# Row normalisation on Trainium2: the size of the DMA descriptors of its loads and stores

## The chip, the cores and the metric

The kernel runs on one core of one Trainium2 chip. The metric is the device time of one launch in microseconds (us). The kernel before the change took 316.64 us as the median of 3 runs (316.41 to 316.7).

## The reference

The input is `x`, 32 x 512 x 1024 numbers in float32 (67.11 MB). Each row of 1024 numbers is divided by the sum of its absolute values:

```python
sums = np.sum(np.abs(x), axis=-1, keepdims=True)
return (x / (sums + 1e-8)).astype(np.float32)
```

Every number is read once and written once, so 134.22 MB must move between the memory (HBM) and the on-chip buffer (SBUF).

## The kernel before

The input is flattened to 16,384 rows of 4,096 bytes. There are 128 SBUF partitions, so each handles 128 rows in all. The rows are cut into eleven tiles: tiles 0 to 9 hold 12 rows per partition (49,152 bytes per partition, 6.29 MB per tile), and tile 10 holds 8 rows per partition (32,768 bytes per partition, 4.19 MB). `piece` (line 33) says which rows a tile holds. Tiles 0, 1 and 10 together are the first 4,096 rows of the input, 32 successive rows per partition; each other tile is a block of 1,536 successive rows, 12 per partition. In every tile the bytes of one partition are contiguous in HBM and in SBUF.

There are four tile buffers (`BUFS = 4`, line 27), and a tile is normalised in place: it is loaded, computed on and stored from the same buffer. The order of the work is written out by hand (lines 108 to 115). Loads of tiles 0 to 3 are issued first. Then, for each tile in turn, `compute(i)` and `store(i)` are issued, and after them `load(i + 4)`, which has to wait until store `i` has landed, because it writes into the same buffer.

Three engines take part:

- SyncE (SP) issues the loads, on its own DMA queue (q1 in the profile), at line 87.
- VectorE (DVE) sums the absolute values of each row (`tensor_reduce`, line 47), adds the epsilon (line 54), takes the reciprocal (line 56) and multiplies most rows (lines 58 and 65).
- ScalarE (ACT) multiplies a few rows of tiles 0, 1, 2, 9 and 10 (line 68) and issues the stores, on its own DMA queue (q10 in the profile), at line 97.

Both queues feed the same 16 DMA engines. A tile is spread evenly over them: 8 of the 128 partitions fall to each engine.

A DMA is made of descriptors, each of which moves one contiguous stretch of bytes; the profile counts and times each of them as one packet, and this text uses that word. `max_dma_last_dim` sets how long, in bytes, such a stretch may be. `HALF` (24,576) is six rows, `WHOLE` (49,152) is twelve rows, and `4 * d` (4,096) is one row. A tile of 12 rows is therefore 128 packets with `WHOLE` and 256 packets with `HALF`; tile 10, with 8 rows, is 128 packets of 32,768 bytes with `WHOLE` and 256 of 16,384 with `HALF`.

The store of tile 0 is issued in two parts: rows 0 to 2 as soon as they are ready, one row per packet (384 packets), and then rows 3 to 11 (128 packets of 36,864 bytes). The store of tile 8 (`last - 2`) is issued in two parts of six rows each, which are 128 packets of 24,576 bytes each whether the limit is `HALF` or `WHOLE`.

In this text "load 4" is the load of tile 4, "store 0a" and "store 0b" are the two parts of the store of tile 0, and "store 8a" and "store 8b" those of tile 8.

Of the kernel before, what the change touches and what calls it, by code (L numbers as in the profile page):

```python
# [1 line left out]

# [4 lines left out]

FP32 = mybir.dt.float32
EPS = 1e-8


@with_exitstack
def kernel(
    ctx: ExitStack,
    tc: tile.TileContext,
    x: bass.AP,
    out: bass.AP,
):
    nc = tc.nc
    P = nc.NUM_PARTITIONS  # L20

    x_flat = x.flatten_outer_dims()
    out_flat = out.flatten_outer_dims()
    n, d = x_flat.shape

    R = 12
    BUFS = 4
    HEAD = 32
    per_partition = n // P
    assert n % P == 0 and (per_partition - HEAD) % R == 0  # L30
    rows = [R] * ((per_partition - HEAD) // R + 2) + [HEAD - 2 * R]

    def piece(flat, i):
        head = flat[: P * HEAD, :].rearrange("(p r) d -> p r d", p=P)
        if i < 2:
            return head[:, R * i : R * (i + 1), :]
        if i == len(rows) - 1:
            return head[:, 2 * R :, :]
        a = P * (HEAD + R * (i - 2))
        return flat[a : a + P * R, :].rearrange("(p r) d -> p r d", p=P)  # L40

    sbuf = ctx.enter_context(tc.tile_pool(name="sbuf", bufs=BUFS))
    stats = ctx.enter_context(tc.tile_pool(name="stats", bufs=len(rows)))

    def normalize(x_tile, k, kv, kt):
        s = stats.tile([P, R], FP32)
        nc.vector.tensor_reduce(  # L47
            out=s[:, :k],
            in_=x_tile[:, :k, :],
            axis=mybir.AxisListType.X,  # L50
            op=mybir.AluOpType.add,
            apply_absolute_value=True,
        )
        nc.vector.tensor_scalar_add(out=s[:, :k], in0=s[:, :k], scalar1=EPS)  # L54
        inv = stats.tile([P, R], FP32)
        nc.vector.reciprocal(out=inv[:, :k], in_=s[:, :k])  # L56
        if kv:
            nc.vector.tensor_mul(  # L58
                out=x_tile[:, :kv, :],
                in0=x_tile[:, :kv, :],  # L60
                in1=inv[:, :kv].unsqueeze(2).to_broadcast([P, kv, d]),
            )
        for r in range(kv, kv + kt):
            row = x_tile[:, r, :]
            nc.vector.tensor_scalar_mul(out=row, in0=row, scalar1=inv[:, r : r + 1])  # L65
        for r in range(kv + kt, k):
            row = x_tile[:, r, :]
            nc.scalar.activation(  # L68
                out=row,
                in_=row,  # L70
                func=mybir.ActivationFunctionType.Copy,
                scale=inv[:, r : r + 1],
            )

    last = len(rows) - 1
    split = {0: (3, 4), 1: (0, 3), 2: (0, 3), last - 1: (0, 2), last: (4, 4)}

    tiles = {}

    HALF, WHOLE = 24576, 49152
    FIRST = 3

    def load(i):
        x_tile = tiles[i] = sbuf.tile([P, R, d], FP32, name="x_tile")
        nc.sync.dma_start(out=x_tile[:, : rows[i], :], in_=piece(x_flat, i), max_dma_last_dim=WHOLE if i < 2 else HALF)  # L87

    def store(i):
        if i == 0:  # L90
            parts = [(0, FIRST, 4 * d), (FIRST, R, WHOLE)]
        elif i == last - 2:
            parts = [(0, R // 2, HALF), (R // 2, R, HALF)]
        else:
            parts = [(0, rows[i], WHOLE if i >= last - 1 else HALF)]
        for a, b, size in parts:
            nc.scalar.dma_start(
                out=piece(out_flat, i)[:, a:b, :],
                in_=tiles[i][:, a:b, :],
                max_dma_last_dim=size,  # L100
            )

    def compute(i):
        k = rows[i]
        kt, ks = split.get(i, (0, 0))
        normalize(tiles[i], k, k - kt - ks, kt)

    with tc.manual_schedule():
        for i in range(BUFS):
            load(i)  # L110
        for i in range(len(rows)):
            compute(i)
            store(i)
            if i + BUFS < len(rows):
                load(i + BUFS)


# [1 line left out]
_INS = ['x']  # L119
_OUTS = [((32, 512, 1024), 'float32')]  # L120


# [23 lines left out]
```

## Time and profile before

| | |
|---|---|
| median of 3 runs | 316.64 us (316.41 to 316.7) |
| span of the profiled execution | 315.2 us |
| bytes read and written | 67.11 MB and 67.11 MB |
| mean DMA rate over the span | 426 GB/s |
| VectorE busy | 260.6 us (83% of the span) |
| ScalarE busy | 18.5 us (6%) |
| DMA packets in all | 5761 |
| load queue q1 | 2736 packets, 49.8% of the 16 engines' span |
| store queue q10 | 3024 packets, 49.4% of the 16 engines' span |

The span is the time from the first to the last recorded instruction or transfer of one execution; the runs' times also hold 1.4 us that lie around it. A packet count of a queue also contains one small packet of 4 bytes per DMA and DMA engine, which reports the landing: 11 loads x 16 = 176, and 13 stores x 16 = 208. So 2736 - 176 = 2560 packets of q1 and 3024 - 208 = 2816 packets of q10 carry data.

The trace also keeps a record of every packet: when it started, how long it was processed, its size and its queue. Some numbers below are from these records. All times of events are in us from the start of the span.

### The profile page before, as it was taken

What the parts mean: (1) busy time and instruction counts of PE and PEld (TensorE: products, weight loads), DVE (VectorE), ACT (ScalarE), POOL (GpSimd) and SP (SyncE); (2) the same over time, 40 slices, a digit from 0 to 9 for tenths busy, and PEclk for the clock granted to TensorE, in tenths of its full rate; (3) what the DMA queues carried; (4) which work ended last, traced back from release to release, by engine and by line L of the source; (5) the groups of instructions that cost most, each with busy time, mean ns of one, the idle gap of its engine ahead of it and who ended that gap; (6) DMA issues with size and microseconds to landing.
All of it is one profiled execution on the core that took longest, in us unless ns stands there. A gap on an engine that the chain in (4) does not pass through costs nothing.

```text
span 315.2 us, 172 instructions
## 1 busy us (share of the span) xinstructions
DVE 260.6 (83%) x50; ACT 18.5 (6%) x17; POOL 0.2 (0%) x4
## 2 busy tenths in 40 slices
DVE  0079999999999999989996997999699969999000
ACT  0010503004000000000000000000000000203200
POOL 0000000000000000000000000000000000000000
DMA  8999999999999999999999999999999999999997
GB/s 318 480 399 412 437 407 464 411 436 413 415 446 437 415 446 437 415 449 434 415 449 437 412 449 437 412 449 437 415 446 437 415 437 434 432 428 496 399 408 324
DMA packets 5761, 134.22 MB, mean 426 GB/s; under 512 B 385, under 2 KB 385, under 8 KB 769
## 3 DMA queue, kind: packets, MB, share of 16 engines
q1 hardware_dynamic: 2736, 67.11, 49.8%
q10 hardware_dynamic: 3024, 67.11, 49.4%
q14 instruction: 1, 0.00, 0.0%
HBM read 67.11 MB, written 67.11 MB: 426 GB/s over the span
## 4 chain that ended last, share of the span: by engine, by line
DVE 40%; DMA 33%; another core or an unknown queue 18%; ACT 1%; issue 0%; SPq 0%
DVE s L47 23%; DMA x_tile<-in_x_dram 17%; DMA out_dram<-x_tile 16%; DVE x_tile L58 15%; ACT x_tile L68 1%; DVE x_tile L65 1%; DVE inv L56 0%; DVE s L54 0%; SPq L87 0%
## 5 line engine op out<-in xcount | busy, mean ns | idle before, releaser
L47 DVE TENSOR_REDUCE s<-x_tile 128x12 f32<-128x12288 f32 (+1 forms) x11 | 138.2, 12562 | 29.8 <-DMA x_tile<-in_x_dram 29.8
L58 DVE TENSOR_TENSOR x_tile<-x_tile,inv 128x12288 f32<-128x12288 f32 (+3 forms) x10 | 113.6, 11358 | 0.5
L68 ACT ACTIVATE x_tile<-x_tile,inv 128x1024 f32<-128x1024 f32 x16 | 17.2, 1138 | 256.9 <-DVE inv L56 256.9
L65 DVE TENSOR_SCALAR x_tile<-x_tile,inv 128x1024 f32<-128x1024 f32 x7 | 4.8, 749 | 0.0
L56 DVE RECIPROCAL inv<-s 128x12 f32<-128x12 f32 (+1 forms) x11 | 2.5, 226 | 0.4
L68 ACT ACT_TABLE_LOAD x1 | 1.3, 1283 | 17.8 <-DMA x_tile<-in_x_dram 17.8
L54 DVE TENSOR_SCALAR s<-s 128x12 f32<-128x12 f32 (+1 forms) x11 | 1.9, 174 | 0.4
L130 POOL MEMSET const-bfloat16-1.0<- 128x1 bf16 x1 | 0.1, 101 | 0.0
L130 POOL MEMSET const-uint8-127<- 128x1 uint8 x1 | 0.1, 101 | 0.0
L130 POOL MEMSET const-float32-0.0<- 128x1 f32 x1 | 0.1, 98 | 0.2 <-issue 0.2
L130 POOL MEMSET const-float32-1.0<- 128x1 f32 x1 | 0.1, 98 | 0.0
## 6 DMA issues: line engine op xcount, KB each, us to landing
x_tile<-in_x_dram SPq DMA_DIRECT2D x10, 6144.0 KB, 36.9
out_dram<-x_tile ACTq DMA_DIRECT2D x8, 6144.0 KB, 49.1
out_dram<-x_tile ACTq DMA_DIRECT2D x2, 3072.0 KB, 33.4
out_dram<-x_tile ACTq DMA_DIRECT2D x1, 4608.0 KB, 37.9
x_tile<-in_x_dram SPq DMA_DIRECT2D x1, 4096.0 KB, 32.2
out_dram<-x_tile ACTq DMA_DIRECT2D x1, 4096.0 KB, 20.9
out_dram<-x_tile ACTq DMA_DIRECT2D x1, 1536.0 KB, 29.3
```

Source lines behind the costliest of these rows:

```text
L47: nc.vector.tensor_reduce(out=s[:, :k], in_=x_tile[:, :k, :], axis=mybir.AxisListType.X, op=mybir.AluOpType.add, apply_absolute_value=True,)
L54: nc.vector.tensor_scalar_add(out=s[:, :k], in0=s[:, :k], scalar1=EPS)
L56: nc.vector.reciprocal(out=inv[:, :k], in_=s[:, :k])
L58: nc.vector.tensor_mul(out=x_tile[:, :kv, :], in0=x_tile[:, :kv, :], in1=inv[:, :kv].unsqueeze(2).to_broadcast([P, kv, d]),)
L65: nc.vector.tensor_scalar_mul(out=row, in0=row, scalar1=inv[:, r : r + 1])
L68: nc.scalar.activation(out=row, in_=row, func=mybir.ActivationFunctionType.Copy, scale=inv[:, r : r + 1],)
L130: nc = _bacc.Bacc("TRN2", target_bir_lowering=False, num_devices=1)
```

## The change

The constant `HALF` goes away, and all loads and stores get the limit `WHOLE`, but for store 0a, which keeps one row per packet. Loads 0 and 1, and stores 0b, 8a, 8b, 9 and 10 keep their packets. Loads 2 to 10 and stores 1 to 7 get packets of twice the size and half their number. No compute instruction changes, and neither does the order of instructions on any engine; the number of DMAs stays at 11 loads and 13 stores.

```diff
-    HALF, WHOLE = 24576, 49152
+    WHOLE = 49152
     FIRST = 3
 
     def load(i):
         x_tile = tiles[i] = sbuf.tile([P, R, d], FP32, name="x_tile")
-        nc.sync.dma_start(out=x_tile[:, : rows[i], :], in_=piece(x_flat, i), max_dma_last_dim=WHOLE if i < 2 else HALF)
+        nc.sync.dma_start(out=x_tile[:, : rows[i], :], in_=piece(x_flat, i), max_dma_last_dim=WHOLE)
 
     def store(i):
         if i == 0:
             parts = [(0, FIRST, 4 * d), (FIRST, R, WHOLE)]
         elif i == last - 2:
-            parts = [(0, R // 2, HALF), (R // 2, R, HALF)]
+            parts = [(0, R // 2, WHOLE), (R // 2, R, WHOLE)]
         else:
-            parts = [(0, rows[i], WHOLE if i >= last - 1 else HALF)]
+            parts = [(0, rows[i], WHOLE)]
         for a, b, size in parts:
```

## The prediction

> **What bounds the kernel now.** I read the page's totals and slices first, then the rate by stretches, the chain that ended last, and the waits.
>
> ```profile
> DMA  8999999999999999999999999999999999999997
> ...
> DMA packets 5761, 134.22 MB, mean 426 GB/s; under 512 B 385, under 2 KB 385, under 8 KB 769
> ...
> q1 hardware_dynamic: 2736, 67.11, 49.8%
> q10 hardware_dynamic: 3024, 67.11, 49.4%
> ```
>
> The two queues together keep the 16 DMA engines busy 99.2% of the span. No slice between the first and the last has a hole. The table of stretches (DVE, ACT and POOL busy, clock, DMA share, GB/s) shows the same:
>
> ```profile
> 62.00:66.00 4.00, 4.00 (x1) 0.00 (x0) 0.00 (x0) 1.00 1.06 393
> 66.00:76.00 10.00, 9.90 (x4) 0.77 (x1) 0.00 (x0) 1.00 1.00 433
> ...
> 110.00:139.07 29.07, 27.54 (x5) 0.00 (x0) 0.00 (x0) 1.00 1.00 433
> 139.07:168.15 29.08, 26.31 (x4) 0.00 (x0) 0.00 (x0) 1.00 1.00 433
> ```
>
> 433 GB/s is the ceiling that mixed loads and stores show over whole periods; 62 to 66 us lies under it. In the last two lines VectorE has 26.3 to 27.5 us of work in 29.1 us, so it is not the bound. The waits say how it idles:
>
> ```profile
> DVE s L47 <- DMA x_tile<-in_x_dram: 29.8, 6, 17.8
> ...
> SPq L87 <- DMA out_dram<-x_tile: 242.1, 8, 63.3
> ```
>
> VectorE waits 17.8 us for the first load and 12 us in all for five later ones; the load queue waits for stores, because a buffer must come free. So the time is a start of 2 us, then the bytes through 16 engines that never rest, then a short end. Only two things can change it: what a packet costs an engine beyond its bytes, and idle or slow engines.
>
> **The merged packets.** Loads 2 to 10 lose 128 packets each (9 x 128 = 1152) and stores 1 to 7 too (7 x 128 = 896): 2048 fewer, 128 per DMA engine. The records give 912 ns for 24,576 bytes and 1815 for 49,152, but on one engine a packet starts 4 ns before the one ahead of it is done: starts are 908 ns apart. The cleanest price is from whole tiles. A load and a store of 16 packets each per engine: load 5 landed at 139.064, load 6 at 168.140 and load 7 at 197.215, so 29.075 us, or 14.5375 per tile and direction. With whole packets: load 1's first packet started at 17.169 and load 2's at 31.669, store 9's at 289.411 and store 10's at 303.911: 14.500 us both times. So 0.0375 us per transfer, 4.7 ns per packet saved. Tile 10's load has smaller packets, but the same number goes away. Sixteen transfers: 16 x 0.0375 = 0.60 us. It is all on the path, since the engines are the bound. If the recorded durations were the cost, with no overlap, it would be 128 x (2 x 912 - 1815) = 1.15 us; from store 8b alone (7.272 us for 8 packets of 24,576 and a report of 9 ns, 907.9 each; whole ones 1811.4) it is 128 x 4.4 = 0.56. I take 0.60 and keep 0.56 to 1.15.
>
> The Trainium skill ("DMA: Bandwidth & Descriptors", Why small descriptors are slow) states about 3 cycles of overhead per packet. At the 850 MHz that the page names, an estimate is 3.5 ns, and 128 x 3.5 = 0.45 us in place of 0.60; the measured 4.7 ns is of that size and decides.
>
> **The first store, 36 to 76 us.** Here the change touches how two queues share an engine. The records show them taking turns packet by packet: from 41 to 62 us each engine alternates one 24,576 of a load and one 4,096 of store 0a (908 + 155 ns). Store 0a was issued at 36.78 and its first packet started at 40.85. The first load needed 1.32 us from issue to first packet (0.73 to 2.05); the other 2.75 us are three load packets of 0.908 that were already lined up. After the change three of 1.811 are, 5.43 us, and up to 1.81 for the running one: store 0a starts between 43.5 and 45.3; I take 44.4. Loads 2 and 3 have 16 packets x 1.811 = 29.0 us from 31.67 on, would end at 60.7, and so have 16.3 us or 9 packets left. Nine pairs of 1.966 us end at 62.1. Of store 0a's 24 packets per engine 15 are then left, alone: 15 x 0.155 = 2.3 us, so 64.4. Before, loads and store 0a ended together at 65.3 to 65.8. Taking turns differently moves no bytes out of the engines' day; what counts is whether the 15 run at 155 ns when alone (second rival).
>
> [...]
>
> **A slow patch.** Load 3's packets average 947 ns and load 2's 919.7, against 912.0 in loads 4 to 9: 16 x 35 + 16 x 7.7 = 0.68 us per engine. Most of it is in two packets per engine started between 62.5 and 64.6 (up to 1600 ns): the 393 GB/s above. It falls where the last load packets meet the last packets of store 0a. No row tells the cause. After the change the mixture lasts 9 pairs instead of 24. Bounds: all 0.68 us saved, or as much lost again. I take 0.2 saved.
>
> **What comes later.** Store 0b needs 10.9 us after 64.4 and lands near 75.6 (before 76.7). Load 4 is issued then, needs 1.32 us, and finds three whole packets of store 1 lined up and part of one running (5.43 + 0.9): first packet at 83.3 instead of 80.77. Taking turns with store 1 and 2 it needs 29.0 us and lands near 112 (before 110.0). VectorE is done with tile 3 at 111.3, so tile 4 starts up to 1 us late, and from tile 5 on every tile waits for its load, as before. Loads then land every 29.0 us, load 9 at 257 (before 255.4). Store 1, served alone for longer, lands near 97 instead of 102.1, so load 5 is queued 15 us ahead of its turn (before 7.8: issued 102.21, load 4 landed 109.99). No queue runs dry. A load 2 to 3 us late costs nothing while the store queue fills the engines. If that cover went, each us late would be a us.
>
> **The end.** This is the chain there:
>
> ```profile
> 218.50 36.97 DMA x_tile<-in_x_dram
> ...
> 255.49 12.96 DVE s L47
> ...
> 268.95 10.82 DVE x_tile L58
> ...
> 279.79 8.70 DVE s L47
> ...
> 288.96 2.79 ACT x_tile L68 x3
> ```
>
> From load 9's landing to the issue of store 10 (293.25) it is 37.8 us; after the change 257 + 37.8 = 294.8. But store 10's first packet started at 303.9, because stores 8a, 8b and 9 were ahead of it. It could be issued as late as 303.9 - 0.6 - 1.3 = 302.0. So 7 us of slack are left, where there were 9 (303.9 - 1.3 - 293.25). Store 9 is issued at 281.4 (before 279.85) and its turn comes near 288.6. The chain that the profile calls last isn't what sets the end: the engines are.
>
> Sum against the profiled span: 315.2 - 0.60 - 0.2 = 314.4. The runs' median is 1.4 us above the span (316.64 against 315.2), so 316.64 - 0.8 = 315.8 us. What this measurement can tell from no change is about 0.2%, 0.63 us.
>
> **Rivals.**
>
> *No visible change.* The packets save their 0.56 to 0.60, but the slow patch stays or grows by up to 0.5 us where longer packets meet 4,096-byte ones: 316.1 to 316.6. For it: the patch's cause is unknown, and a patch per load stays possible. Against: fewer pairs meet.
>
> *Slower, by small packets alone.* After the loads have ended, 15 packets per engine of 4,096 bytes run with nothing between them until 0b, and each may cost more than 155 ns if the engine can't overlap them. For it: seven instruction packets of 8,192 bytes, each on a queue that was otherwise empty, took 361 to 549 ns (median 493). At half of that, 247, it is 15 x 92 ns = 1.4 us more: 317.2. At a full 493 each, 5.1 us: 320.9. Against: where two such packets follow each other at 47 us, the second starts 155 to 161 ns after the first. It decides from 250 ns per packet.
>
> *Slower, by long packets in turn.* No row has a whole load beside a whole store. If 128 of them per engine cost what the first load's did (mean 1907 instead of 1815, with the engines just started), it is 128 x 0.092 = 11.8 us: 327.8. Against: whole loads alone and whole stores alone keep 14.500, and ten tiles of half packets in turn show 912.0 to 912.1.
>
> *The change does nothing,* if the hardware cuts packets anyway: 316.6. Against: the records of loads 0 and 1 show 49,152 bytes in one.
>
> **How the numbers follow.** Forecast 0.56 (315.1 to 316.3); no visible change by the patch 0.20; small packets alone 0.15; long packets 0.06; nothing done 0.03. Faster by over 0.2% is under 316.0: four fifths of the forecast's chance and a little of the first rival, 0.47. Within 0.2%: the rest of these two and the last, 0.32. Slower: the two rivals, 0.21. Range: below, 316.64 - 0.60 - 0.68 = 315.4, and 0.3 lower if packets cost somewhat more than 4.7 ns; above, up to 317.6, small packets alone at 275 ns. That leaves about 0.1 above and 0.05 below.
>
> **What would show it.** The page should count 3713 packets (q1 1584, q10 2128). Loads 5 to 9 should land 29.00 us apart instead of 29.075; VectorE's waits per tile grow little. Load 4's first packet should be near 83, store 10's issue near 295 with its first packet near 303. Store 0a should end some 2 us after load 3, its last packets 155 ns apart. I am wrong if a slice before the last shows the DMA under full, if 4,096-byte packets come slower than 155 ns, or if whole packets in turn take more than 1811.

## The result, and the profile after

The changed kernel took 319.9 us (median of 5 runs, 318.78 to 323.17) against 316.56 us (5 runs, 316.41 to 316.7): a ratio of 1.0113, with a 95% interval of 1.0066 to 1.0159. It became 1.1% slower where 0.8 us less were forecast, and its runs now scatter over 4.4 us where those of before lie within 0.3. The traced run is the longest of the five, 323.17 us with a span of 321.5 us, so it shows the loss at its largest. Of the experiments below, one run of e12 (323.0 us, its traced one) and one of e14 (324.87 us) lie over 1.5% above the fastest run of their kernel, count as slow for that, and are left out of the medians and ranges.

From the page of the changed kernel (the DMA share in 40 slices, GB/s in the same slices, packets, the two queues, and VectorE's sums with the idle time before them):

```profile
span 321.5 us, 172 instructions
...
DMA  8999999999999999999999999999999999999980
GB/s 349 434 404 477 391 432 424 384 472 440 416 465 391 483 397 477 397 428 452 391 483 397 477 397 452 428 391 483 391 477 404 444 432 405 433 456 401 448 371 20
DMA packets 3712, 134.22 MB, mean 417 GB/s; under 512 B 384, under 2 KB 384, under 8 KB 768
...
q1 hardware_dynamic: 1584, 67.11, 48.8%
q10 hardware_dynamic: 2128, 67.11, 48.3%
...
L47 DVE TENSOR_REDUCE s<-x_tile 128x12 f32<-128x12288 f32 (+1 forms) x11 | 138.2, 12561 | 34.0 <-DMA x_tile<-in_x_dram 34.0
```

The two queues have the packets that were expected (1584 and 2128), 3712 in all where 3713 were forecast, since no instruction packet falls into this span. The first 38 slices are full. What is new is the last slice: 8 us with 20 GB/s. The table of stretches puts it next to the stretch ahead of it (DVE, ACT, POOL, clock, DMA share, GB/s):

```profile
300.00:312.00 12.00, 0.00 (x0) 0.00 (x0) 0.00 (x0) 1.00 0.96 416
313.00:314.50 1.50, 0.00 (x0) 0.00 (x0) 0.00 (x0) 1.00 0.10 44
314.50:320.50 6.00, 0.00 (x0) 0.00 (x0) 0.00 (x0) 1.00 0.05 22
```

Before the change no packet of data started behind 313 us:

```profile
300.00:313.00 13.00, 0.00 (x0) 0.00 (x0) 0.00 (x0) 1.00 1.01 436
313.00:315.20 2.20, 0.00 (x0) 0.00 (x0) 0.00 (x0) 1.00 0.00 0
```

One of 16 engines is a share of 0.06 and, of 433 GB/s, 27 GB/s. So from 314.5 us on about one DMA engine is still at work. The reports, which are in the packet records, say it exactly, since each engine reports its own part of a DMA. A packet record doesn't name its engine; which packets belong to one engine is worked out here from each one starting where another ends. These are the times at which the 16 engines reported load 5, load 9 and the last store, and the lag of the last one behind the median:

| reports | first | median | second latest | last | lag of the last |
|---|---|---|---|---|---|
| before, load 9 | 254.30 | 254.75 | 255.36 | 255.36 | 0.6 |
| before, last store | 313.59 | 313.80 | 314.05 | 314.14 | 0.3 |
| after, load 5 | 137.66 | 137.84 | 138.12 | 140.20 | 2.4 |
| after, load 9 | 253.66 | 253.85 | 254.31 | 259.61 | 5.8 |
| after, last store | 312.94 | 313.12 | 314.56 | 320.56 | 7.4 |

Fourteen engines have finished by 313.24 us, before the first one did before (313.59), and the median engine is 0.68 us earlier, where 0.8 was forecast. One engine falls behind by a little in each tile and finishes 7.4 us after the median; a second one is 1.4 us late. VectorE, the load queue and the end of the kernel all wait for the last engine, because a tile has landed only when all 16 parts have. The Trainium skill ("DMA: Bandwidth & Descriptors", Why a DMA increments its semaphore by 16 and not by 1) states that the engines finish independently and only the full count means that the data has landed; the trace agrees, with 253.66 us for the first and 259.61 us for the last report of one load.

The lag is made of single packets that take longer than their size. I call a packet stretched if it took over 30 ns more than usual for its size (1815 ns for 49,152 bytes, 912 for 24,576). After 104 us the trace of before has none among all its packets; the trace after has 26, by 33 to 1311 ns, 8.2 us in all. Chained by their times, about 7 us of this are on the last engine and 1.1 us on the second latest.

### The profile page after: what moved, and what is told of

The parts are those of the page before. It is cut to its first block, busy times and chain, and to the rows that moved or that the text cites. A ratio compares the mean times of both kernels' runs of the same rounds, so it can differ in the third digit from the quotient of the medians.

```text
span 321.5 us, 172 instructions
## 1 busy us (share of the span) xinstructions
DVE 260.5 (81%) x50; ACT 18.5 (6%) x17; POOL 0.2 (0%) x4
## 2 busy tenths in 40 slices
DMA packets 3712, 134.22 MB, mean 417 GB/s; under 512 B 384, under 2 KB 384, under 8 KB 768
## 3 DMA queue, kind: packets, MB, share of 16 engines
q1 hardware_dynamic: 1584, 67.11, 48.8%
q10 hardware_dynamic: 2128, 67.11, 48.3%
## 4 chain that ended last, share of the span: by engine, by line
DMA 32%; DVE 31%; another core or an unknown queue 28%; ACT 1%; issue 0%; SPq 0%; ACTq 0%
DVE s L47 19%; DMA x_tile<-in_x_dram 17%; DMA out_dram<-x_tile 14%; DVE x_tile L58 11%; ACT x_tile L68 1%; DVE x_tile L65 1%; DVE inv L56 0%; SPq L85 0%; DVE s L54 0%; ACTq L95 0%
```

## The experiments

The table has what the runs of each kernel took, and from its one traced run the stretched packets after 104 us and the reports of the last store (for e12 the traced run is the one that its median leaves out). The median engine shows what the packets cost in themselves; the last engine shows what falls behind.

| kernel | us, median (range) | stretched: number, sum in us | last store: median, last engine |
|---|---|---|---|
| before | 316.56 (316.41 to 316.7) | 0, 0 | 313.80, 314.14 |
| changed | 319.9 (318.78 to 323.17) | 26, 8.2 | 313.12, 320.56 |
| e1, whole loads only | 323.48 (322.12 to 323.87) | 324, 72.6 | 318.48, 320.88 |
| e2, whole stores only | 324.08 (323.11 to 326.7) | 140, 48.2 | 320.38, 320.48 |
| e3, quarter packets | 317.76 (317.51 to 318.46) | 0, 0 | 314.75, 314.93 |
| e4, store 0a in 12,288 | 317.17 (315.89 to 319.87) | 16, 2.9 | 313.07, 314.74 |
| e5, store 0 in one | 317.57 (316.6 to 320.67) | 4, 0.6 | 313.94, 314.70 |
| e6, half, store 0a in 12,288 | 316.48 (316.3 to 316.89) | 0, 0 | 313.49, 313.71 |
| e7, copy, whole | 316.14 (316.08 to 317.01) | 2, 0.2 | 313.21, 313.53 |
| e8, copy, half | 316.87 (316.68 to 317.04) | 0, 0 | 313.98, 314.08 |
| e9, copy, whole, VectorE busy | 316.19 (315.99 to 316.96) | 3, 0.2 | 313.36, 313.59 |
| e10, copy, whole, extra work on 8 engines | 318.37 (317.79 to 318.44) | 0, 0 | 314.02, 315.83 |
| e11, whole, order only | 317.17 (316.44 to 319.24) | 5, 1.3 | 313.27, 314.45 |
| e12, whole, order and reads | 318.79 (316.7 to 319.74) | 28, 7.5 | 313.32, 320.39 |
| e13, copy, whole, 1 engine far behind | 346.6 (343.47 to 347.24) | 89, 27.1 | 320.56, 340.93 |
| e14, copy, half, 1 engine far behind | 321.25 (318.97 to 321.58) | 12, 0.5 | 316.82, 319.05 |
| e15, whole, extra work on 8 engines | 318.6 (318.52 to 319.85) | 1, 0.1 | 314.29, 315.96 |
| e16, half, 1 engine far behind | 319.87 (319.8 to 320.0) | 1, 0.05 | 313.64, 317.34 |
| e17, copy, whole, extra work on 2 engines | 319.68 (318.34 to 319.83) | 40, 6.6 | 313.22, 317.10 |
| e18, copy, half, extra work on 2 engines | 317.73 (317.57 to 317.78) | 0, 0 | 314.12, 315.01 |

### Which packets: e1 to e4

e1 takes half packets for stores 1 to 7 of the changed kernel, e2 for its loads 2 to 10.

```diff
-            parts = [(0, rows[i], WHOLE)]
+            parts = [(0, rows[i], WHOLE if i >= last - 1 else 24576)]
```

> Whole packets (49,152 bytes) for the loads only; stores 1 to 7 stay at half packets. In the changed kernel 14 DMA engines ended 0.6 us earlier than before, as packets saved promise, and one engine fell behind by 7.4 us, a little at a time, between 109 and 284 us. Theory A (an engine falls behind when whole loads and whole stores take turns): no engine ends more than 1 us after the others, 316.6 - 9 x 0.0375 = 316.2 us. Theory B (whole loads are enough, since nearly all long packets were loads): one engine ends 2 to 7 us after the others, 318 to 323 us. Theory C (whole stores do it): as theory A.

```diff
-... max_dma_last_dim=WHOLE)
+... max_dma_last_dim=WHOLE if i < 2 else 24576)
```

> Whole packets for the stores only; loads 2 to 10 stay at half packets. Theory A (both directions needed): no engine ends more than 1 us late, 316.6 - 7 x 0.0375 = 316.3 us. Theory B (whole loads): the same, 316.3 us. Theory C (whole stores): one engine 2 to 7 us late, 318 to 323 us.

Theory A fell at once: one direction alone is worse than both, 323.48 and 324.08 us. Theories B and C, with one late engine, don't describe it either. In e1 the median engine itself ends 4.7 us later than before, and 324 packets are stretched, 72.6 / 16 = 4.5 us per engine. Half packets beside whole ones are stretched too: 51 of the 324 in e1, by up to 709 ns, and 33 of the 140 in e2, by up to 1184 ns, have 24,576 bytes. In e2 there is a second loss. The queues take turns by packets, so the queue with packets of twice the size gets two thirds of the bytes. The loads get one third, load 4 lands at 121.95 us instead of 109.99, and near the end the store queue is empty. This is the DMA share and GB/s in slices of e2's page:

```profile
DMA  8999999999999999999999999999999999994997
GB/s 318 465 391 440 440 408 457 400 449 440 440 391 440 434 446 425 422 428 483 440 425 401 450 404 422 431 394 431 401 422 431 419 404 415 434 438 213 489 391 326
```

The slice with 213 GB/s is engines that wait at 294 us for store 9, which VectorE has not released yet. Part of this wait is stretching again: the last engine reported load 9 at 270.49 us, 3.6 us after the median one, and VectorE starts on tile 9 only then. The cover that the prediction relied on at the end is gone there.

e3 takes quarter packets (12,288 bytes) in loads 2 to 9 and stores 1 to 7.

> Loads 2 to 9 and stores 1 to 7 in packets of 12,288 bytes (load 10 at 16,384 as before). The packet price of 4.7 ns says 15 transfers x 8 partitions x 2 more packets per engine = 240 x 4.7 ns = 1.1 us more than before: 317.7 us, with all engines ending within 0.6 us. If long packets cost by their length alone (theory D: every halving helps, the half packets of before also lose something), it is below 317.2 us.

317.76 us against 317.7 worked out: the price of 4.7 ns per packet holds, and theory D, which needed less than 317.2 us, is out.

e4 is the changed kernel with `(0, FIRST, WHOLE)` in place of `(0, FIRST, 4 * d)`.

> The changed kernel with store 0a in 128 packets of 12,288 bytes instead of 384 of 4,096. If the small packets beside whole loads start the trouble (theory E: they put one engine out of step), no engine ends more than 1 us late and it is 315.8 us. If whole loads and stores in turn do it on their own (theories A to C), one engine still ends 2 to 7 us late: 318 to 323 us.

Both theories are half right. The best run, 315.89 us, is near the forecast of 315.8, but the others reach 319.87. With the 4,096-byte packets the trouble is larger (319.9 us against 317.17), but it is there without them.

### What it takes: e5 to e12

e5 is the changed kernel with the store of tile 0 as one DMA.

```diff
-        if i == 0:
-            parts = [(0, FIRST, 4 * d), (FIRST, R, WHOLE)]
-        elif i == last - 2:
+        if i == last - 2:
```

> The changed kernel with the store of tile 0 as one DMA of 128 whole packets, so that no size other than 49,152 bytes is in use from 17 to 257 us. Theory F (engines that are in step stay in step; other sizes put single engines out of step, and then their load packets are stretched): packets of one size throughout leave all engines within 1 us of each other at the end, and every run takes 315.9 us (316.6 - 0.6), within 0.3. Theory G (long packets in turn do it on their own, at random): 317 to 320 us with a scatter of over 1 us, and in the trace one engine that ends 1 to 7 us late.

One size throughout does not keep the engines in step, nor the runs within 0.3 us, so theory F fails: 317.57 us, 316.6 to 320.67. In its trace the load packets at 41 to 46 us, when the first store begins, are stretched by 21 us summed over the engines. After that the engines report load 2 in two groups, 7 at 51.3 to 51.7 us and 9 at 52.8 to 53.2. They stayed apart, but from 104 us on there are only 4 stretched packets, and no single engine is late as theory G has it.

e6 is the kernel before with `(0, FIRST, WHOLE)`.

> The kernel before (half packets), with store 0a in 128 packets of 12,288 bytes instead of 384 of 4,096. The slow patch at 62 to 66 us cost the kernel before 0.6 us; the kernel with whole packets and this store (e4) has none. If the 4,096-byte packets make the patch, it is gone here and the time is 316.6 - 0.6 - 16 x 0.0047 = 315.9 us. If the patch has another cause, it stays: 316.5 us. Half packets show no engine falling behind either way.

The slow patch at 62 us is gone from its trace, yet the runs are the same as before (0.9999, interval 0.999 to 1.0007). The packet records show that most of the stretching has moved, not gone. Summed over the engines, the packets of loads 2 and 3 take 10.9 us over their usual time before (2.0 in load 2, 9.0 in load 3), and 7.8 us in e6, all in load 2 at 39 to 47 us, when the first store begins. That is 0.2 us less per engine, not 0.6. The trace of e4, which was read above as having no patch, has 10.5 us in load 2. Why load packets are stretched at these times isn't shown.

e7 and e8 are the changed kernel and the one before without `compute(i)`: tiles are loaded and stored as they are.

> The changed kernel without any computation: each tile is loaded and stored as it is. If VectorE or ScalarE at work, or their starting at a landing, stretches the packets (theory H), no engine falls behind and this is 0.6 us under its twin with half packets (e8). If it lies between the DMA queues and memory alone (theories F and G), one or more engines end 1 to 7 us late, and this is 1 to 7 us over e8.

> The kernel before without any computation, the twin of e7. All theories: no engine falls behind; loads and stores fill the engines from 2 us on as before, so 314 to 317 us, with all engines ending within 0.6 us.

Here whole packets win 0.73 us, the saving that was forecast, with the engines within 0.6 us of each other throughout. So whole loads and whole stores in turn are not slow in themselves (theory G is out), and the loss needs something that this copy lacks.

e9 adds sums over a scratch row to e7, which depend on nothing.

```diff
+        for i in range(22):
+            nc.vector.tensor_reduce(out=total[:, :], in_=row[:, :].unsqueeze(1).to_broadcast([P, R, d]), ...)
```

> The copy with whole packets and no computation (e7, 316.1 us), with VectorE at work for 285 us on a scratch row of its own: 22 sums like those of line 47, which wait for no load and for which no store waits. If VectorE's use of the buffer stretches packets (theory H), one or more engines end 1 to 7 us late and the time is 317 to 323 us. If it takes the kernel's own order of events, that is stores that wait for the computation (theory J), it stays at 316.1 us, within 0.3.

316.19 us: VectorE at work on a buffer of its own does not matter, and with it theory H is out as far as VectorE goes; ScalarE at work was not tried alone. e10 gives 8 of the 16 engines extra work in the same copy.

```diff
         for i in range(BUFS):
             load(i)
+        for j in range(2):
+            nc.sync.dma_start(out=pad[8 * j : 8 * j + 8, :], in_=x_flat[24 * j : 24 * j + 24, :].rearrange(...), max_dma_last_dim=WHOLE)
```

> The same copy with whole packets and no computation, with 2 more loads of 8 partitions x 12,288 bytes behind the first four loads. They add 0.91 us of work to 8 of the 16 engines (or less to all of them, if they are spread) and put these half a packet behind the others. Theory F (engines out of step have their long load packets stretched): the trace shows stretched packets after 65 us and the time is over 317.3 us. If being out of step is harmless without the computation (theories H and J): 316.1 + 0.9 = 317.0 us at most, with the two groups a constant 0.9 us apart.

The time passed theory F's mark, but not for its reason: there is no stretched packet after 104 us. The last store is reported by 8 engines up to 313.62 us and by the other 8 from 314.41 to 315.83. Of the extra 2.2 us, 0.9 are work; another part is a patch at 66 to 72 us, when the extra loads ran (6.0 us summed over the engines).

e11 and e12 keep the order of events of the changed kernel. VectorE waits for the load, works as long as it did, and releases the store; it touches one number per partition in place. In e11 the work is done on a scratch row, in e12 on the tile, which it only reads.

> The changed kernel with VectorE's work replaced by sums of the same lengths over a scratch row; in each tile VectorE only multiplies one number per partition by 1 before and after them, so that it waits for the load and the store waits for it, as in the changed kernel. ScalarE computes nothing, and the output is the input. If the order of events makes single DMA engines fall behind (theory J: loads and stores that are released by the computation's end and by the last engine's landing), the time is 318 to 323 us with one or more engines 2 to 7 us late. If it needs the computation to read or write the tile buffers (theory K), the time is 315.9 to 316.4 us, as in the copy (e7).

> As e11, but the sums run over the tile itself, so that VectorE reads the tile buffers all the time and writes single numbers only. Theory J: 318 to 323 us, as e11. Theory K by reads: 318 to 323 us with e11 at 316. Theory K by writes (the multiplication in place): 315.9 to 316.4 us, both here and in e11.

e11 lies between the two theories: 317.17 us, up to 319.24. e12 lies between e11 and the changed kernel, at 318.79 us. Its traced run, of 323.0 us, which its median leaves out, looks like the changed kernel's: one engine alone, with load 5 last reported at 140.18 us, load 9 at 259.79 and the last store at 320.39. Since runs of one kernel scatter by about 3 us, these two don't tell how much reading the tiles adds to the order.

### One engine alone: e13 to e18

In the traces of the changed kernel and of e4 it was one or two engines that fell behind fourteen or more. e13 puts one engine out of step by an extra load, in the copy with whole packets; e14 does the same in the copy with half packets, e16 in the kernel before.

```diff
         for i in range(BUFS):
             load(i)
+        nc.sync.dma_start(out=pad[:, :], in_=x_flat[:17, : d // 2])
```

> The copy with whole packets and no computation (e7, 316.1 us), with one more load of 17 partitions x 2,048 bytes behind the first four loads. If it falls to one DMA engine alone (17 is odd), it adds 17 x (75 + 5) ns = 1.4 us to that engine's work. Theory L (one engine alone out of step with the others has its packets stretched, again and again): that engine falls further behind, 319 to 323 us, as in the changed kernel. Theory J alone (it takes the computation between load and store): 316.1 + 1.4 = 317.5 us at most, the lag constant.

> The same extra load on one engine in the copy with half packets (e8, 316.9 us). All theories that need whole packets: the lag stays at up to 1.4 us and the time is at most 318.3 us. If a lone engine is held up at any packet size: 319 us or more.

> The kernel before (half packets, with the computation) with the extra load on one engine. If half packets are safe: 316.6 to 318.0 us, the lag of that engine constant from 80 us on. If computation and a lone late engine are enough at any packet size: 319 us or more with a growing lag.

The extra load was larger than meant. All its 17 packets of 2,048 bytes fell to one engine, but each waited its turn behind a packet of the store queue, so that engine's loads were set back far more than 1.4 us: it reported load 4 17.8 us after the median of the others in e13 (126.80 us against 108.98), 20.5 us in e14 and 6.4 us in e16. So the times of e13, e14 and e16 all lie above what was expected; in e14 and e16 the whole lag arose up to 104 us. What tells is what the engine does afterwards, when the small packets are done. These are stretches of e7 (copy, whole packets, all in step), e13 and e14 (POOL, clock, DMA share, GB/s):

```profile
104.00:160.00 56.00, 0.00 (x0) 1.00 1.01 435
160.00:220.00 60.00, 0.00 (x0) 1.00 1.00 433
220.00:290.00 70.00, 0.00 (x0) 1.00 1.00 431
```

```profile
104.00:160.00 56.00, 0.00 (x0) 1.00 1.01 432
160.00:220.00 60.00, 0.00 (x0) 1.00 1.00 428
220.00:290.00 70.00, 0.00 (x0) 1.00 0.97 418
290.00:320.00 30.00, 0.00 (x0) 1.00 0.82 353
321.00:341.00 20.00, 0.00 (x0) 1.00 0.06 25
```

```profile
104.00:160.00 56.00, 0.00 (x0) 1.00 1.01 434
160.00:220.00 60.00, 0.00 (x0) 1.00 1.00 433
220.00:290.00 70.00, 0.00 (x0) 1.00 1.01 437
```

With whole packets the lone engine never recovers: about every second of its packets is stretched, by up to 1487 ns, to 290 us, and the last 20 us of e13 are that engine alone at 25 GB/s. Its distance to the others grows from 17.8 us in load 4 to 22.0 in load 5 and 26.2 in load 6. With half packets the engine is as far out of step (e14), but nothing is stretched by over 50 ns from 104 us on, it is still 20.5 us behind in load 9 (in e16 still 6.4), and the rate is that of e7.

e15 is the changed kernel, computation and all, with the two extra loads of e10.

> The changed kernel with the two extra loads of e10, which in the copy put two groups of engines 1 to 2.5 us apart and cost 2.2 us (0.9 us of work and a stretch at 66 us). Theory L: with two groups no engine is alone; no lag grows after 80 us, and the time is 318.4 us, like e10, with a scatter under 1 us. Theory J alone: single engines fall behind on top of it, 319 to 325 us with a scatter of several us.

318.6 us against 318.4 expected, though with a scatter of 1.3 us and not under 1, and one stretched packet after 104 us: no single engine drifts away. But the reports don't show 8 late engines here. Twelve engines report load 4 at 110.5 to 111.7 us and four at 112.5 to 112.8, and these four are as far behind in load 9.

e17 is a milder version of e13: the loads of e10 cut to two partitions each, which add 0.9 us of work to two engines. e18 does the same with half packets.

> The copy with whole packets and no computation (e7, 316.1 us), with 2 more loads of 2 partitions x 12,288 bytes behind the first four loads, which make two DMA engines 0.9 us late (e10 did the same to eight). Theory L (few engines out of step with many are held up in whole packets): the two fall further behind, with stretched packets after 104 us, and it is 318 to 323 us. If it takes a lag as large as in e13, or the computation: 317.1 us at most and a constant lag.

> The same two late engines in the copy with half packets (e8, 316.9 us). Theory L: half packets are not held up; no stretched packet after 104 us, 317.8 us at most.

These are the ends of e17 and of e18 (POOL, clock, DMA share, GB/s):

```profile
313.00:314.50 1.50, 0.00 (x0) 1.00 0.25 109
314.50:318.00 3.50, 0.00 (x0) 1.00 0.02 9
```

```profile
313.00:314.50 1.50, 0.00 (x0) 1.00 0.11 44
314.50:318.00 3.50, 0.00 (x0) 1.00 0.00 0
```

e17 shows it with a smaller lag and without computation: 40 stretched packets after 104 us. Not two but five engines are 1.3 to 2.7 us behind the median in load 4. The last engine is 2.7 us behind there (111.66 us against 108.94), 5.1 us in load 9 and 3.9 us at the end. In its half twin e18 the two engines are 4.5 us behind in load 4 and 4.5 us behind in load 9, no packet is stretched, and the last one ends 0.9 us behind, as much as its extra work: 317.73 us against at most 317.8 expected.

So what theory L says of few engines against many is not shown: four behind twelve were not stretched in e15, five behind eleven were in e17, from one traced run each.

No kernel with the whole computation beat the one before beyond its interval.

## Why the prediction was wrong

- **What bounds the kernel** was right for fourteen engines: they are full to their end, and the chain with VectorE has slack. Store 10 was issued at 297.34 us (294.8 forecast), and its first packet started at 303.3 (near 303 forecast).
- **The merged packets** were right in price: 0.60 us forecast; the median engine's last report came 0.68 us earlier, 0.73 us were measured between the copies e7 and e8, and e3 was slower by 1.2 us where 1.1 was worked out. That all of it is on the path was not, since the last engine decides.
- **The first store** was wrong in a detail that cost nothing: store 0a started at 41.03 us and not at 44.4, so what is lined up ahead is not three packets of any size. Twelve small packets, not 15, were left alone, from 63.3 us on. They started 155 ns apart, so the rival of slow small packets is refuted.
- **The slow patch** was wrong: 0.2 us were taken as saved, and nothing was. Load 3's excess fell from 9.0 to 4.6 us summed over the engines, but load 2's rose from 2.0 to 6.6, so 10.9 us became 11.2.
- **What comes later** held on the median engine: it reported loads 5 to 9 29.0 us apart. Load 4 landed at 109.3 us, not 112, in part because its first packet came at 81.4 us and not at 83.3.
- **The step that failed** is the sentence that taking turns differently "moves no bytes out of the engines' day", and with it the reading of the bound as 16 engines that never rest and end together. The working was done for one engine and taken for all. The runs showed that with whole packets in turn an engine that has lost its step with the others can be held up packet by packet, and that the kernel ends with that engine: 7.4 us late in the trace, and 3.3 us more in the median than before. The prediction named the sign, whole packets in turn that take more than 1811 ns.
- **The rival of long packets in turn** (chance 0.06) named the right place, a whole load beside a whole store, which no row of before showed. Its price was wrong in kind: not every packet 92 ns longer on all engines (11.8 us), but few packets, up to 1311 ns longer, nearly all on one engine. The row that it was refused by, ten tiles of half packets at 912.0, said nothing about whole ones.

Shown by the runs: whole packets and engines put out of step are enough, without any computation (e17, 319.68 us, against the copy in step, e7, 316.14, and against its half twin e18, 317.73). One lone engine is not needed for a loss, since in e1 all 16 engines ended after the last one of before. Not shown: why such a packet is held up, why the engines out of step in e5, e10 and e15 were spared, and what first sets one engine back in the changed kernel. The copies stayed in step (e7, e9), kernels in which the stores wait for VectorE mostly did not (e11, e12, the changed one), and with the small packets of store 0a it was worse (e4); how these act together is open.

## What to carry to other kernels

A transfer over 16 DMA engines ends with the slowest of them, so look at the engines' separate reports, not only at the DMA share of the span: here 97% of it was full while one engine decided the end. Merging packets saved 4.7 ns for each one less, 0.2% in all, but here, with both directions full, the kernel as a whole became 1.1% slower; runs that suddenly scattered by over 1% were the sign. Two queues share an engine by packets, so unequal sizes share it unequally (e2: loads with one third of the bytes).

## What was not expected of the hardware

- A packet of 49,152 bytes on an engine out of step was stretched by up to 1487 ns (e13), while the kernels whose loads and stores both had packets of 24,576 or of 12,288 bytes in the middle had none over 50 ns after 104 us (before, e3, e6, e8, e14, e16, e18). Beside whole packets half ones were stretched too, by up to 1184 ns (e2).
- Engines out of step with whole packets are stretched in some traces and not in others: 0, 1 and 4 stretched packets after 104 us in e10, e15 and e5, against 26 to 89 in the changed kernel, e17 and e13. What decides isn't shown.
- Seventeen packets of 2,048 bytes on one engine (35 KB) cost 30 us of the whole kernel's time when they took turns with whole packets (346.6 us against 316.14), and 4.4 us with half packets (321.25 against 316.87).
